# Another machine model for the scheduler that orders a two-block kernel's instructions

## The chip, the cores and the metric

The kernel runs on one core of a Trainium2 chip. The metric is the time of one execution on the device, in microseconds. The three runs shown before the change took 2196.48, 2199.58 and 2181.83 us, with a median of 2196.48.

## The reference

One sequence of 256 tokens with 1024 features goes through two blocks of two layers each. Block 1 puts 16 meta tokens in front (272 in all). Each of its layers computes

```
proj = h @ w_in                       # q k v z b a | sq sk sv | iq ik iw
o_dn = gated_delta_rule(q, k, v, ...) # convolution, chunks, a state passed on
score = sum_h relu(iq_h ik^T) iw_h    # 8 indexer heads
sel   = top_k(causal(score), 64)      # 64 keys for each query
o_sa  = attention of sq over the selected keys, 8 heads
h = layer_norm(a*h + concat(o_dn, o_sa) @ w_out)
h = layer_norm(a*h + moe(h))          # 32 experts, 2 per token
```

Block 2 drops the meta tokens. Each of its layers takes the sum of three gated branches (block-sparse attention with 8 heads, chunked gated linear attention with 4 heads, attention into a memory of 256 tokens), a projection, and an MLP of 4096 with a squared ReLU. All in float32.

## The kernel before

Weights come in from memory as they are used, 414.9 MB for one execution, through the SP queue. Tokens stay on the chip. A product to float32 accuracy is made of three matmuls, L240, L241 and L242: weights and activations are each split into a high and a low part (ScalarE at L232 makes the high part, VectorE at L233 the low one). In block 1 such a product is [128 features x 272 tokens] wide; in block 2 mostly 512.

Block 1, one layer. The projections of q, k, v come first, then the convolution and the delta rule: L932 to L1057 prepare the chunks, with L976 doubling a triangular inverse step by step, and L1067 to L1098 pass the state through them. The indexer's queries and keys are projected and rotated (L496 on TensorE, L499 on VectorE). For two tiles of 128 queries, L522 makes the scores of 8 heads, ScalarE applies the ReLU, and L526 adds them on VectorE. Eight rounds of L531 (the eight largest) and L532 (strike them out) find 64 keys; L533 and L535 turn that into an additive mask, `bias`. The projections of sq, sk and sv, four weights of 256 columns in two pieces each, are written beside the indexer in the program. The sparse heads follow: L627 is the product of queries and keys, L629 adds the mask by a matmul, L630 takes the maximum, L637 and L641 transpose the probabilities, L648 and L650 multiply by the values, and L653 divides by the sums and writes `osa`. In layer 0 the 16 meta tokens have their own heads (L584 to L606). The memory of block 2 is prepared on the side (L1577 on VectorE scales it, L1583 transposes it, L1595 loads its weights).

The expert weights go through three rings of tiles (L1113 loads w1 and w3, eight tiles of 1 MB for a group of four experts; L214 loads w2). The first ring is free during the heads; the second lies where the heads' tiles are, so its loads wait for their end. There are eight groups of four experts a layer: L1186 gathers tokens, L1197 is the first product, L1208 a transpose, L1216 the second product, L1225 scatters.

In block 2, L1783 is a chain of the linear attention: six levels of masks, each of which waits for masked copies on VectorE (L1818) and factors made by ScalarE, VectorE and GpSimd (L1800).

No order of the instructions is written out. The program is a sequence of calls, and the framework's list scheduler puts the instructions of each engine in an order of its own before it places waits between engines. That scheduler picks by a model of the machine. Each engine then executes its list in order, and SP issues the DMAs in its list in order.

Of the kernel before, what the change touches and what calls it, by code (L numbers as in the profile page):

```python
# [15 lines left out]
PSUM = bass.MemoryType.PSUM  # L16
# [4 lines left out]
CAP = 32  # L21
# [19 lines left out]
def _consts():  # L41
    """Tables that depend on the shapes alone: masks, identities, rotary tables of block 1."""
# [64 lines left out]
def build(tc, A, out, dbg=None, stop=None):  # L107
    nc = tc.nc
    es = ExitStack()
    with es:  # L110
# [9 lines left out]
        # the memory's keys and values, and scratch, for the whole run  # L120
        K.pt = es.enter_context(tc.tile_pool(name="mem0", bufs=1, side="right"))
        K.mem = {0: mem_tiles(K, K.pt)}
        for l in range(2):
            with ExitStack() as st:
# [17 lines left out]
                # the expert weights start to come in beside the output projection  # L142
# [5 lines left out]
            with ExitStack() as st:  # L148
                # what dies first lies where the next phase starts
                K.pe = st.enter_context(tc.tile_pool(name="moee%d" % l, bufs=1))  # L150
                K.pf = st.enter_context(tc.tile_pool(name="moef%d" % l, bufs=1))
                K.wc = st.enter_context(tc.tile_pool(name="wringc%d" % l, bufs=RC))
                K.p = st.enter_context(tc.tile_pool(name="moe%d" % l, bufs=1))
                b1_moe(K, l)
# [12 lines left out]
        # block 2: what is needed first lies on the right, where the expert weights were  # L167
# [15 lines left out]
# tiles of the three rings of expert weights; up to which weight of a group the first two serve  # L183
# [20 lines left out]
def wcols(K, w, c0, n=256):  # L204
    """Columns c0.. of a [1024, N] weight as [128, 8, n]."""
# [5 lines left out]
def wrows(K, w, r0, nk=2):  # L211
    """Rows r0.. of a [K, 1024] weight as [128, nk, 1024]."""
# [5 lines left out]
def split(K, x, shape, pool=None):  # L218
    """A float32 weight block of up to 1024 columns as an exact sum of two float32r blocks."""
# [17 lines left out]
def mm3(K, out, a, b, start, stop):  # L237
    """out += a^T b to float32 accuracy; a and b are (high, low) pairs."""
# [6 lines left out]
def put(K, dst, src, sl):  # L245
    """Writes src (PSUM or SBUF) as a high and a low part."""
# [14 lines left out]
def setup(K):  # L261
# [23 lines left out]
    # the convolutions' taps as columns  # L285
# [4 lines left out]
    # a_log, dt_bias on all partitions  # L290
# [14 lines left out]
def feature_columns(K):  # L305
    """The other vectors over features as columns."""
# [9 lines left out]
def to_T(K, src, t):  # L316
    """One token-major tile -> feature-major high and low parts."""
# [10 lines left out]
def row_bank(K, k, tag):  # L328
    """512 features from column k of K.lcol on, along a row that is the same on all partitions."""
# [6 lines left out]
def interleave(gens):  # L336
    """Runs generators in turn, one step of each, until all are done."""
# [9 lines left out]
def yield_from(gen):  # L347
    """Runs a generator to its end and gives what it returns."""
# [7 lines left out]
def b1_attention(K, l, mix, st):  # L356
# [55 lines left out]
    # small columns: db, da, iw  # L412
# [147 lines left out]
    # the memory of block 2 and the first expert weights come in early  # L560
# [13 lines left out]
def b1_sparse_meta(K, sqT, skT, vtok, mix):  # L574
    """The 16 meta tokens, all heads at once."""
# [85 lines left out]
def router_weights(K, l, p):  # L661
    """Router weights with the norm's gain on them, high and low parts; the norm's bias goes with theirs."""
# [19 lines left out]
def b1_project(K, l, mix):  # L682
    """Output projection, residual, layer norm, router logits and choices."""
# [30 lines left out]
    def norm(t, halves):  # L714
        """Residual and norm before gain and bias (left in K.y); feature-major parts of it for the router."""
# [67 lines left out]
def norm_stats(K, y, P, ss, junk, at=0):  # L783
    """Minus the mean and the inverse deviation of y [P, 1024] into ss[:, 2] and ss[:, 5]; ss[:, 0:2] holds the half sums."""
# [16 lines left out]
class Route:  # L801
    """Grouped top-2 routing, one token tile after the other: the expert slots of the tokens and their gates."""
# [26 lines left out]
    def choose(self, t):  # L829
        """The two experts of each token."""  # L830
# [18 lines left out]
    def rank(self, t):  # L849
        """The token's rank among those of the expert."""  # L850
# [9 lines left out]
    def gates(self, t):  # L860
        """Half of the gates of a token tile."""
# [16 lines left out]
class Delta:  # L878
    """Gated delta rule on one token tile: two chunks of 64, or the 16 meta tokens."""
# [12 lines left out]
    def pre(self):  # L892
# [42 lines left out]
        # normalised keys and queries, feature-major  # L935
# [33 lines left out]
        # T = (1 + L)^-1 by block doubling; U its transpose  # L969
# [37 lines left out]
        # token-major keys and values  # L1007
# [101 lines left out]
def moe_load(K, l, g, n):  # L1109
    """Weight n of a group of four experts: w1 of each, then w3 of each."""  # L1110
# [11 lines left out]
def b1_moe(K, l):  # L1122
    """Tokens are gathered into CAP slots per expert; tokens past the slots of an expert take a dense path in a loop
    that only runs when an expert has any."""
# [12 lines left out]
    # the first group's loads began beside the projection  # L1137
# [9 lines left out]
    def onehot(g):  # L1147
        """Token -> slot of a group's experts."""
# [5 lines left out]
    def gates(g, oh):  # L1154
        """The gates there."""
# [4 lines left out]
    def gated(og_):  # L1160
        """Gated slot -> token."""
# [9 lines left out]
    def gain(dst, src, k):  # L1171
        """The first norm's gain and bias of feature block k."""
# [65 lines left out]
    # the meta tokens' sums lie beside them  # L1238
# [3 lines left out]
    def init():  # L1242
        """The residual, of the normed tokens."""
# [30 lines left out]
    # tokens without a slot  # L1274
# [21 lines left out]
def moe_overflow(K, l, ovf, acc, rows, tiles, gain):  # L1296
    """Adds the contribution of the tokens that found no slot, whatever their number."""
# [3 lines left out]
    with tc.If(n > 0):  # L1301
        # tokens feature-major, and the gates of those past the slots
# [45 lines left out]
def setup2(K):  # L1348
    """Per-feature vectors of block 2."""
# [30 lines left out]
def setup2_rest(K):  # L1380
    """Masks, gains on token-major heads, and rotary tables."""
# [872 lines left out]
```

## Time and profile before

| | us |
|---|---|
| runs: median, lowest, highest | 2196.48, 2181.83, 2199.58 |
| the profiled execution: span from first to last instruction | 2178.1 |
| block 1, layer 0: attention; experts | 0 to 316; 325 to 587 |
| block 1, layer 1: attention; experts | 600 to 886; 887 to 1141 |
| block 2, layer 0 | 1148 to 1664 |
| block 2, layer 1 | 1664 to 2178 |

The profile is of one execution. Its own time is not among the three runs; its span lies 3.7 us below the lowest of them and 18.4 below the median. In rows of the trace a busy TensorE is a modelled one: matmuls are pipelined, so what counts is when the next one starts. PEclk is the granted TensorE clock, 1.00 for 2.4 GHz and 0.50 for 1.2.

### The profile page before, as it was taken

To read this page: it belongs to the slowest core of one execution; us is meant where nothing else is said; L and a number is where in the kernel's file an instruction comes from. 1 tells how busy PE (TensorE), PEld (TensorE's weight loads), DVE (VectorE), ACT (ScalarE), POOL (GpSimd) and SP (SyncE) were. 2 spreads that over 40 slices of the span, in tenths; PEclk is the share of its full clock that TensorE was granted. 3 is DMA by queue.
4 is the path that set the end of the run, shared out by engine and by line. 5 is a ranking of instruction groups with operands and counts; after the bars stand their busy time and mean duration, and the time that the engine had idled before them with its cause. 6 is when DMAs were issued, how large, how long until landed. Compare 5 with 4: busy or idle time off the path is not lost. (4 is left out here: it accounts for less than half of the span.)

```text
span 2178.1 us, 34809 instructions
## 1 busy us (share of the span) xinstructions
PE 2037.9 (94%) x14216; PEld 1588.2 (73%) x14216; DVE 1091.5 (50%) x2179; ACT 762.0 (35%) x1478; POOL 358.9 (16%) x342
## 2 busy tenths in 40 slices
PE   8999999999699999988768999999999999999999
PEld 7888665544299887543326779889878869898987
DVE  6658444221376583521116674555545575555554
ACT  5214322111242243211015434455534524445543
POOL 1325000000022430000001130123400031122410
PEclk9999799999899997999889899999999989999999
DMA  7304288999942154999995243254555434244553
GB/s 220 97 20 136 78 290 297 340 356 371 301 132 74 44 187 141 344 368 366 365 335 170 83 166 120 88 184 155 173 194 163 133 116 146 88 153 145 168 193 116
DMA packets 321670, 414.90 MB, mean 190 GB/s; under 512 B 25480, under 2 KB 277970, under 8 KB 321506
## 3 DMA queue, kind: packets, MB, share of 16 engines
q1 hardware_dynamic: 315110, 410.85, 56.4%
q8 instruction: 114, 1.87, 0.4%
q10 hardware_dynamic: 6396, 1.77, 0.3%
q14 instruction: 50, 0.41, 0.1%
HBM read 411.54 MB, written 1.05 MB: 189 GB/s over the span
## 5 line engine op out<-in xcount | busy, mean ns | idle before, releaser
L233 DVE TENSOR_TENSOR wl<-w,wh 128x1024 fp32r<-128x1024 f32 x329 | 411.5, 1253 | 270.8 <-ACT wh L232 263.5
L232 ACT CAST wh<-w 128x1024 fp32r<-128x1024 f32 x350 | 365.7, 1047 | 429.8 <-PE ps_d L241 251.3
L240 PE MATMUL ps_d<-hh,wh 128*128 128x256 f32 (+1 forms) x1632 | 481.7, 296 | 5.5 <-ACT tg L2161 1.9
L242 PE MATMUL ps_d<-hh,wl 128*128 128x256 f32 (+1 forms) x1632 | 475.1, 291 | 0.3
L241 PE MATMUL ps_d<-hl,wh 128*128 128x256 f32 (+1 forms) x1632 | 475.0, 291 | 0.0
L240 PEld LDWEIGHTS ps_d<-hh,wh 128*128 128x128 f32 x1632 | 310.1, 190 | 17.4 <-issue 6.4
L242 PEld LDWEIGHTS ps_d<-hh,wl 128*128 128x128 f32 x1632 | 310.6, 190 | 9.1 <-DVE wl L233 6.9
L241 PEld LDWEIGHTS ps_d<-hl,wh 128*128 128x128 f32 x1632 | 310.1, 190 | 4.7 <-issue 0.8
L1197 PE MATMUL ps_d<-wb,hg 128*32 128x256 f32 x2048 | 156.0, 408 | 33.1 <-DMA wb<-in_w 33.0
L1197 PEld LDWEIGHTS ps_d<-wb,hg 128*32 128x32 f32 x2048 | 73.4, 117 | 106.5 <-DMA wb<-in_w 43.4
L2221 POOL TENSOR_TENSOR relu<-relu 128x256 f32<-128x256 f32 x64 | 86.6, 1354 | 129.6 <-ACT relu L2220 129.6
L1186 PE MATMUL ps_c<-oh,y 128*128 128x128 f32 (+1 forms) x640 | 101.9, 297 | 0.0
L1201 DVE SCALAR_TENSOR_TENSOR mth<-mth,ps_d 128x256 f32<-128x256 f32 x16 | 6.7, 421 | 183.5 <-ACT mth L1200 183.4
L1186 PEld LDWEIGHTS ps_c<-oh,y 128*128 128x128 f32 (+1 forms) x640 | 82.7, 189 | 21.1 <-issue 5.7
L1216 PE MATMUL ps_d<-w,hid 128*32 128x512 f32 x512 | 80.9, 637 | 12.1 <-ACT hid L1210 7.9
L795 POOL TENSOR_TENSOR lnst<-lnst,nhalf 128x1 f32<-128x1 f32 (+1 forms) x5 | 4.9, 980 | 479.7 <-DVE lnst L794 477.8
L1228 DVE TENSOR_TENSOR yacc<-yacc,ps_c 128x512 f32<-128x512 f32 x56 | 38.5, 687 | 83.6 <-PE ps_c L1225 83.6
L1200 ACT ACTIVATE mth<-ps_d 128x256 f32<-128x256 f32 x16 | 6.1, 383 | 211.5 <-PE ps_d L1197 211.5
L233 POOL TENSOR_TENSOR wl<-w,wh 128x1024 fp32r<-128x1024 f32 x21 | 50.0, 2383 | 129.2 <-ACT wh L232 119.8
L2175 POOL TENSOR_TENSOR mergedT<-mergedT,tg 128x256 f32<-128x256 f32 x32 | 32.6, 1041 | 234.0 <-DVE tg L2173 234.0
L1216 PEld LDWEIGHTS ps_d<-w,hid 128*32 128x32 f32 x512 | 21.7, 115 | 60.3 <-issue 36.8
L1225 PE MATMUL ps_c<-ysl,ohT 128*128 128x512 f32 (+1 forms) x140 | 64.5, 603 | 0.0
(679 smaller groups left out, 3686.1 us busy)
## 6 DMA issues: line engine op xcount, KB each, us to landing
wb<-in_w SPq DMA_DIRECT2D x128, 1024.0 KB, 12.0
w<-in_w_in SPq DMA_DIRECT2D x82, 1024.0 KB, 5.3
w<-in_w SPq DMA_DIRECT2D x64, 1024.0 KB, 11.4
w<-in_w_up SPq DMA_DIRECT2D x32, 1024.0 KB, 5.3
w<-in_w_down SPq DMA_DIRECT2D x32, 1024.0 KB, 4.9
w<-in_w_out SPq DMA_DIRECT2D x16, 1024.0 KB, 4.8
w<-in_w_branch SPq DMA_DIRECT2D x24, 512.0 KB, 4.2
w<-in_mem_w_kv SPq DMA_DIRECT2D x8, 1024.0 KB, 5.7
```

Source lines behind the costliest of these rows:

```text
L232: K.nc.scalar.copy(h, x)
L233: eng.tensor_tensor(lo, x, h.bitcast(F32), op=OP.subtract)
L240: PE.matmul(out, a[0], b[0], start=start, stop=False, skip_group_check=True)
L241: PE.matmul(out, a[0], b[1], start=False, stop=False, skip_group_check=True)
L242: return PE.matmul(out, a[1], b[0], start=False, stop=stop, skip_group_check=True)
L1186: PE.matmul(ps[:, (k % 4) * 128:(k % 4) * 128 + 128], y[t][:P, k * 128:(k + 1) * 128], oh[:P, t, :], start=(i == 0), stop=(i == nt - 1))
L1197: PE.matmul(pu[j * 32:j * 32 + 32, i * 256:i * 256 + 256], hg[:, k, j * 32:j * 32 + 32], wts[i][j][:, k, :], start=(k == 0 and i == 0), st ...
L1216: PE.matmul(ps[q * 32:q * 32 + 32, :], hid[:, j, q * 32:q * 32 + 32], w2t[q][:, j, hf * 512:(hf + 1) * 512], start=(j == 0), stop=(j == 1) ...
L1225: PE.matmul(ps[rows[t]], ohT[:, off:off + P], ysl[:, hf * 512:(hf + 1) * 512], start=True, stop=True)
L1228: V.tensor_tensor(sl, sl, ps[rows[t]], op=OP.add)
L2175: G.tensor_tensor(m, m, tg, op=OP.add)
L2221: G.tensor_tensor(r, r, r, op=OP.mult)
```

## The change

The list scheduler takes its times from the framework's detailed simulation of the machine, in place of a simple one. The rest of the diff takes out comments and docstrings; the lines keep their numbers, and no instruction is added or removed on purpose.

```diff
-    with tile.TileContext(nc) as tc:
+    with tile.TileContext(nc, schedule_with_timeline_sim=True) as tc:
         build(tc, A, out)
```

What moves is seen in the order of each engine's list, in nearly all of it. Three places follow, in which x2 means two in a row and "..." rows left out.

**TensorE, layer 0, from the indexer's first scores (L522) to the heads (L627).** Before, the scores stand in eight pairs, each followed by some eight products (L240 to L242) and a rotation (L496), here the first pair and the head of the second:

```order
L522 MATMUL ps_c<-ikT,iqT 128x144 x2
L240 MATMUL ps_d<-hh,wh 128x272
L241 MATMUL ps_d<-hl,wh 128x272
L242 MATMUL ps_d<-hh,wl 128x272
...
L496 MATMUL ps_o<-rraw,cst_750 128x272
...
L522 MATMUL ps_c<-ikT,iqT 128x144 x2
```

Now:

```order
L242 MATMUL ps_d<-hh,wl 128x272
...
L1067 MATMUL ps_c<-state,uw_1285 128x128 x4
L1071 MATMUL ps_p<-state,qd_874 64x128 x4
L1086 MATMUL ps_p<-uw_1285,AT_921 128x128 x4
L1098 MATMUL ps_c<-cst_91,don 128x128 x4
L522 MATMUL ps_c<-ikT,iqT 128x144 x8
L522 MATMUL ps_c<-ikT,iqT 128x272 x8
L1583 MATMUL ps_o<-cst_91,memx 128x128
L1583 MATMUL ps_p<-cst_91,memx 128x128
L553 MATMUL ps_c<-cst_91,rraw 128x128 x2
L553 MATMUL ps_c<-cst_91,rraw 16x128
```

All products that stood between and behind the pairs are now ahead of the first L522, between steps of the delta rule; the last steps of the state (L1067 to L1098) and the sixteen scores stand in one piece. After row L627 come more of the memory's transposes, nine matmuls of the output projection, and then L629 of the first head, in which the mask is added. Layer 1 has the same order, with seven and one of the larger scores.

**VectorE, layer 0, the eight rounds over the larger tile.** Before:

```order
L532 MATCH_REPLACE iacc<-m_2230,iacc 128x272
L531 MAX m_2230<-iacc 128x8
L233 TENSOR_TENSOR wl<-w,wh 128x1024
L532 MATCH_REPLACE iacc<-m_2230,iacc 128x272
...
L233 TENSOR_TENSOR wl<-w,wh 128x1024
...
L533 TENSOR_SCALAR iacc<-iacc 128x272
L535 TENSOR_TENSOR bias_2248<-iacc,cst_750 128x272
L1585 TENSOR_TENSOR memT<-ps_o,lcol 128x512
...
L233 TENSOR_TENSOR wl<-w,wh 128x1024
```

Now:

```order
L531 MAX m_2230<-iacc 128x8
L532 MATCH_REPLACE iacc<-m_2230,iacc 128x272
L533 TENSOR_SCALAR iacc<-iacc 128x272
L535 TENSOR_TENSOR bias_2248<-iacc,cst_750 128x272
L630 TENSOR_REDUCE sst<-ps_d 128x1 x3
L631 TENSOR_SCALAR sst<-sst 128x1 x3
```

Before, weight splitting (L233) stands between the rounds; now nothing of the projections is left there, and L535 is followed directly by the heads' L630 and L631.

**TensorE, block 2, layer 0, inside the chain L1783.** Before:

```order
L1783 MATMUL ps_c<-gX 128x128 x2
L241 MATMUL ps_d<-wl,hh 128x512
L1783 MATMUL ps_c<-gX 128x128 x6
L242 MATMUL ps_d<-wh,hl 128x512
L240 MATMUL ps_d<-wh,hh 128x512
L241 MATMUL ps_d<-wl,hh 128x512
L1783 MATMUL ps_c<-gX 128x128 x2
L242 MATMUL ps_d<-wh,hl 128x512
L1783 MATMUL ps_c<-gX 128x128 x6
```

Now:

```order
L1783 MATMUL ps_c<-gX 128x128 x2
L242 MATMUL ps_d<-hh,wl 24x256
L240 MATMUL ps_d<-hh,wh 24x256
L241 MATMUL ps_d<-hl,wh 24x256
...
L1783 MATMUL ps_c<-gX 128x128 x2
L242 MATMUL ps_d<-hh,wl 24x256
L240 MATMUL ps_d<-hh,wh 24x256
L241 MATMUL ps_d<-hl,wh 24x256
L1783 MATMUL ps_c<-gX 128x128 x2
...
L240 MATMUL ps_d<-wh,hh 128x512 x2
```

Before, up to six matmuls of the chain stand in a row with one to eight of a weight product between; now they stand in twos and fours with three to eleven matmuls of other products between, and the chain begins later in the list.

On the SP queue the expert weights keep their pattern (eight tiles at L1113, then four at L214), with up to two tiles more of L1113 ahead of an L214. The pools and rings are the same.

## Rows read from the trace of the kernel before

**Rows 1.** The page: span, and TensorE's busy us, share, instructions.
```profile
span 2178.1 us, 34809 instructions
...
PE 2037.9 (94%) x14216; PEld 1588.2 (73%) x14216; DVE 1091.5 (50%) x2179; ACT 762.0 (35%) x1478; POOL 358.9 (16%) x342
```

**Rows 2.** Table by stage: stretch, length, busy us per engine (count), granted clock, DMA.
```profile
12.00:172.00 160.00, 152.76 (x1255) 142.08 (x1255) 102.77 (x228) 51.29 (x93) 47.23 (x33) 0.99 0.35 103
172.00:221.00 49.00, 46.78 (x331) 41.13 (x330) 43.26 (x90) 23.30 (x52) 24.52 (x23) 1.00 0.45 153
222.00:243.00 21.00, 21.00 (x124) 14.89 (x123) 10.11 (x35) 9.12 (x33) 0.00 (x0) 0.99 0.41 130
243.00:275.00 32.00, 32.00 (x122) 20.02 (x122) 8.94 (x32) 5.44 (x21) 0.00 (x0) 0.53 0.00 0
325.00:587.00 262.00, 240.50 (x1823) 120.06 (x1822) 71.79 (x164) 35.99 (x86) 2.03 (x2) 0.97 0.98 337
604.00:760.00 156.00, 150.00 (x1226) 140.18 (x1225) 100.59 (x217) 48.28 (x89) 44.10 (x31) 0.98 0.25 77
806.00:826.00 20.00, 20.00 (x118) 14.03 (x116) 9.47 (x34) 8.61 (x32) 0.00 (x0) 1.00 0.78 257
826.00:850.00 24.00, 24.00 (x84) 17.34 (x83) 6.22 (x22) 4.97 (x21) 0.00 (x0) 0.50 0.00 1
886.00:1141.00 255.00, 210.60 (x1704) 103.42 (x1704) 56.47 (x137) 35.67 (x85) 2.03 (x2) 0.93 1.04 358
```

**Rows 3.** Waits of SP's DMA queue, 760 to 870: total us, times, longest.
```profile
SPq L1113 <- DVE osa L653: 36.7, 1, 36.7
```

**Rows 4.** Groups of PE instructions: 172 to 222 us, then 759.6 to 803.
```profile
L240 PE MATMUL ps_d<-hh,wh 128*128 128x272 f32 x88 | 27.0, 307 | 0.0
...
L496 PE MATMUL ps_o<-rraw,cst 128*128 128x272 f32 x16 | 5.7, 435 | 2.2 <-DVE rt L499 1.3 <-ACT rraw L494 0.7
...
L240 PE MATMUL ps_d<-hh,wh 128*128 128x272 f32 x84 | 25.7, 306 | 0.0
```

**Rows 5.** Timelines of PE and DVE, pieces: start us, length us, engine, line.
```profile
170.83 0.29 PE L240 MATMUL ps_d<-hh,wh 128*128 128x272 f32 x1
...
171.83 0.28 PE L242 MATMUL ps_d<-hh,wl 128*128 128x272 f32 x1
172.04 0.52 PE L522 MATMUL ps_c<-ikT,iqT 64*128 64x144 f32 x4
...
174.60 0.53 DVE L526 SCALAR_TENSOR_TENSOR iacc<-irel,wis,cst 128x144 f32<-128x144 f32 x1
...
220.33 0.44 DVE L535 TENSOR_TENSOR bias<-iacc,cst 128x272 bf16<-128x272 f32 x1
...
759.64 0.52 PE L522 MATMUL ps_c<-ikT,iqT 64*128 64x144 f32 x4
...
802.36 0.44 DVE L535 TENSOR_TENSOR bias<-iacc,cst 128x272 bf16<-128x272 f32 x1
```

**Rows 6.** Groups of DVE instructions, 172 to 222 us.
```profile
L233 DVE TENSOR_TENSOR wl<-w,wh 128x1024 fp32r<-128x1024 f32 x9 | 12.1, 1341 | 1.8 <-ACT wh L232 1.8
...
L499 DVE TENSOR_TENSOR rt<-ps_o,cst 128x272 f32<-128x272 f32 x8 | 3.4, 428 | 0.0
```

**Rows 7.** Table by stage: the end of expert layer 0.
```profile
587.00:591.00 4.00, 0.95 (x6) 0.77 (x7) 3.26 (x7) 3.08 (x6) 1.31 (x2) 0.96 1.10 349
591.00:604.00 13.00, 8.92 (x51) 7.37 (x50) 11.36 (x17) 5.51 (x9) 4.15 (x5) 0.50 0.72 181
```

**Rows 8.** Waits of PE, whole span: total us, times, longest.
```profile
PE ps_d L1197 <- DMA wb<-in_w: 33.0, 17, 2.5
...
PE ps_c L1783 <- DVE gAT L1818: 6.1, 6, 1.8
```

**Rows 9.** Table by stage: around the chain L1783 in block 2.
```profile
1239.00:1253.00 14.00, 14.00 (x55) 9.91 (x52) 8.48 (x19) 2.24 (x4) 2.40 (x3) 0.51 0.12 39
1751.00:1762.00 11.00, 11.00 (x39) 7.52 (x37) 7.32 (x16) 2.13 (x4) 2.40 (x3) 0.53 0.01 3
```

## The prediction

> **What bounds the kernel now.** I read the page first: TensorE (PE) is busy 94% of the 2178.1 us span [rows 1], so a new order can do two things only: open or close gaps on PE, and change the clock at which PE runs. That average hides three kinds of stage, so next came the table by stage. The projections, the delta rule and block 2 are limited by PE itself: 152.76 busy of 160 in attention before the indexer, 46.78 of 49 while it runs, 150.00 of 156 in layer 1 [rows 2]. The expert stages are limited by transfers (337 and 358 GB/s at a DMA share of 0.98 and 1.04). Between them stand the sparse heads, a chain of small steps through PE, VectorE (DVE) and ScalarE (ACT), where PE looks fully busy but the granted clock is 0.99 in the first 21 us and 0.53 in the next 32; in layer 1 it is 1.00, then 0.50 [rows 2]. 1.00 is 2.4 GHz and 0.50 is 1.2. DMA is still there (0 and 1 GB/s): the next expert weights go into memory that the heads' tiles hold, and in layer 1 the SP queue waits 36.7 us for the heads' last result [rows 3]. So the end of the heads is on the path: whatever delays it delays the expert loads as well, and those set the length of the next stage.
>
> **Top-k loses its cover.** In the old order the products that score keys (L522) stand in eight pairs between the remaining projections. While DVE takes the 64 best keys, PE works those off. In the new order all of these projections stand before the first L522, between steps of the delta rule. After L522 PE has left only transposes of the memory (L1583, L553), one product per head as far as three banks go, and nine products of the output projection, before L629 needs the mask.
>
> Layer 0, step by step. What moves ahead of L522: three lines of x88, x88 and x89 (one is shown), 265 products, and 16 rope products [rows 4]. Eight products in sequence take from 170.83 to 171.83, that is 0.125 us each [rows 5]: 33.1 us. The ropes are of the same width and overlap their neighbours (5.7 us busy); I count 0.2 each, 3.2. That is 36.3 in all. They are put where PE now has 160 - 152.76 = 7.2 us of idle time [rows 2]; I let them fill all of it. The first L522 comes at 172.04 now [rows 5], hence at 172.0 + 36.3 - 7.2 = 201.1. DVE begins 174.60 - 172.04 = 2.6 us later [rows 5]. DVE is busy 43.26 us from there to the mask [rows 2]; weight splitting (L233, 12.1) and the rotations (L499, 3.4) lie in it now and are gone from it in the new order [rows 6]: 27.8 stay, the rounds L531 and L532 and the memory's L1577 among them, one after another. The mask is ready at 201.1 + 2.6 + 27.8 = 231.5. It is ready now at 220.33 + 0.44 = 220.8 [rows 5]: **+11 us**. Lower end +7, if the memory's part falls into other gaps; upper end +16, if the delta rule's waits stay and the ropes cost all of their 5.7.
>
> Layer 1 has three lines of x84, x84 and x83 between its first L522 at 759.64 and its mask at 802.36 + 0.44 [rows 4, 5]: 251 products, 31.4, and 3.0 for ropes, less 6.0 idle us [rows 2], start L522 at 788.0. With 2.6 + 27.8 the mask comes at 818.4, +16. DVE's chain is some us shorter there (its splitting and the rest fit into 43 us beside it), so I take **+13**; ends 7 and 19.
>
> **The clock of the heads.** Rows show heads starting at 1.00 right after dense products, then falling to 0.50 some 20 us in, and staying there [rows 2]. Elsewhere a stretch with little on PE goes the same way: in the second layernorm 0.95 us busy of 4 is followed by 13 us at 0.50 [rows 7]. In the new order some 20 us with nearly empty PE come just before the heads, so I expect them to begin at 0.50. Price from the rate of instructions: layer 0 has 124 in 21 us at full clock and 122 in 32 at half [rows 2], so 124 at the half-clock rate take 32.5 us, +11.5; layer 1, 118 in 20 and 84 in 24, gives +13.7. The two parts do not hold the same mix, so I take **+10 per layer**. Ends: 0, if the clock stays up, and +20, if the first part doubles.
>
> The Trainium skill, TensorE: Matmul & The Clock Gate, section on HAM oscillation, says that waits which leave the engine idle let its clock fall, so that the next burst starts cold. That speaks against this change. By it the heads begin cold in both layers, and the sum below would be +48, with the upper ends of 20 in place of 10. The trace agrees in the layernorm, where the clock falls to 0.50; no row of it shows heads that begin so.
>
> **Delta rule.** It gets the projections as filler. That gain is already used: the 7.2 and 6.0 idle us above. Its PE work is unchanged.
>
> **Expert stages.** The new order puts the next group's first product (L1197) between the scatter products (L1225), and the SP queue brings w2 as before behind each eight tiles of w1 and w3. The transfers bound the stage, and none is added. I cost it at **0**. Below: layer 0 at layer 1's 358 GB/s would take 262 x 337 / 358 = 246.6, -15 us. Above: PE now executes in order behind a tile that may be late; one wait of about 1 us for each of 16 groups gives +16, which is half as long as the present waits for these tiles, 33.0 us in 17 times [rows 8].
>
> **Block 2.** The chain L1783 waits for DVE (6.1 us for two layers) [rows 8], and its clock drops: 14 us at 0.51 and 11 us at 0.53 [rows 9]. At full clock these would take about 7 and 6, so at most -7 - 3 and -5 - 3 with the waits, **-18** for both. The new order starts it later and puts three to eleven products between every two or four of its own, where six stood in a row. I take -8 each, **-16**; the other end is 0. The rest of block 2 is saturated in both orders.
>
> **Sum.** 11 + 13 for the mask, 2 x 10 for the clock, 0 for the experts, -16 for block 2: +28 on the profiled execution, 2178.1 to 2206. That execution is 18.4 below the median of the three runs, 2196.48, and 3.7 below the lowest, 2181.83. On the median the forecast is 2224.5, **2225 us**.
>
> **Rivals.**
> - *The clock holds.* The nine products and L1583 keep PE awake, or the heads run as now. Then 24 - 16 = +8: 2204, within 1%. For it: the heads of today stay at 1.00 for 20 us with small work. Against: during top-k almost nothing is left for PE. Chance 0.31, which takes in that the new order changes nothing that matters (2196), and a forecast that comes out a little smaller.
> - *Faster: expert loads start inside the heads.* The DMA is idle there for 32 and 24 us [rows 2]. If the new order frees the tiles that those loads wait for before the heads end, the transfer-bound stages that follow shorten by up to 56. With 24 + 20 - 16 that gives -28: 2168. It decides from 50 of those 56 us on (28 + 22), or from 30 on if the clock holds too (8 + 22). Against it: the pools are as before, and the wait is for the heads' own last result [rows 3]. Chance 0.15, and 0.07 for a sum of smaller gains (layer 0's expert stage -15, the clock held, the mask only +7).
> - *The forecast*, slower: 0.47.
>
> About 1% (22 us) is what a measurement tells from no change. Faster by over 1%: 0.22; within: 0.31; slower: 0.47. The range: the ends of all terms together are 14 + 0 - 15 - 18 = -19 and 35 + 40 + 16 + 0 = +91. With the second rival the lower end is -28, 2168. The upper is cut at +70, 2267, since the high ends do not all come together. The forecast's own range is 2205 to 2267.
>
> **What would show it.** Right: in the new trace the larger tile's L535 ends near 231 and 816, PE is nearly empty for 15 to 25 us before, the heads begin at 0.50, the expert loads begin some 20 us later in each layer, and L1783 loses its half-clock stretch. Wrong: a granted clock of 1.00 at the start of the heads; a mask no later than now; expert loads that start before the heads are done; an expert stage longer or shorter by over 15 us.

## The result and the profile after

The changed kernel took 2256.85 us (median of four runs, 2255.80 to 2261.32), the kernel before 2191.97 beside it (2181.83 to 2199.58). The ratio is 1.031, with an interval from 1.027 to 1.035: slower by 65 us, where I had forecast slower by 28. The side was right, the size was not.

The page of the changed kernel: span, TensorE, and the granted clock in 40 slices.

```profile
span 2254.0 us, 34907 instructions
...
PE 2068.6 (92%) x14216; PEld 1612.1 (72%) x14216; DVE 1094.9 (49%) x2179; ACT 763.7 (34%) x1478; POOL 364.6 (16%) x342
...
PEclk9998588998989996799889899999999999999999
```

The number of PE instructions is that of before [rows 1], and PE is busy 31 us longer in a span that is 76 us longer. The 31 are a balance: by the tables further down, block 2 is busy 21 us less, so block 1 is busy 52 us longer, and PE also idles some 46 us longer there. Both count: longer busy time (the 5 and the 6 in the line PEclk lie at the heads of the two layers) and waiting.

The table by stage of the kernel after, with the columns of [rows 2]: layer 0 up to the scores, the top-k, the heads in two parts, the expert groups; then layer 1 up to the heads' second part.

```profile
12.00:214.00 202.00, 191.54 (x1539) 179.79 (x1539) 121.11 (x244) 66.26 (x117) 65.88 (x52) 0.99 0.35 108
214.00:241.00 27.00, 18.66 (x77) 13.45 (x76) 24.38 (x78) 10.41 (x35) 2.38 (x3) 0.69 0.59 195
241.00:262.00 21.00, 19.42 (x62) 11.74 (x61) 6.10 (x25) 6.53 (x23) 0.00 (x0) 0.50 0.00 0
262.00:291.00 29.00, 28.20 (x115) 21.29 (x115) 8.21 (x32) 6.06 (x24) 0.00 (x0) 0.50 0.00 1
...
375.00:631.00 256.00, 233.88 (x1791) 116.15 (x1784) 64.39 (x140) 32.57 (x80) 0.00 (x0) 0.96 0.97 333
```

```profile
656.00:851.00 195.00, 186.44 (x1502) 176.27 (x1503) 115.83 (x233) 62.62 (x110) 64.14 (x49) 0.98 0.30 94
851.00:879.00 28.00, 19.74 (x77) 13.47 (x77) 24.59 (x77) 10.41 (x35) 2.57 (x3) 0.69 0.58 188
879.00:903.00 24.00, 22.48 (x72) 13.74 (x71) 6.76 (x26) 6.90 (x24) 0.00 (x0) 0.50 0.00 1
903.00:923.00 20.00, 19.20 (x70) 14.82 (x70) 5.84 (x22) 5.11 (x21) 0.00 (x0) 0.50 0.00 0
```

Against [rows 2]: while VectorE picks the keys, PE has 77 instructions in 27 us, where it had 331 in 49. The heads begin at a granted clock of 0.50, where they began at 0.99 and 1.00. In layer 0 the clock is 0.50 from 240.5 to 291.7, 51.2 us; before, from 242.6 to 273.3, 30.7 us. In layer 1 it is 44.4 us, and was 23.9.

Milestones in the timelines of after (start us, length us, engine, line): the first scores, the mask and the last head of layer 0, the last expert product of layer 0, and the same of layer 1.

```profile
214.64 3.29 PE L522 MATMUL ps_c<-ikT,iqT 64*128 64x144 f32 x14
240.57 0.44 DVE L535 TENSOR_TENSOR bias<-iacc,cst 128x272 bf16<-128x272 f32 x1
300.64 0.69 DVE L653 TENSOR_TENSOR osa<-ps_o,sst 128x512 f32<-128x512 f32 x1 [4.88 <-PE ps_o L650]
630.26 1.06 PE L1216 MATMUL ps_d<-w,hid 128*32 128x512 f32 x8
851.41 0.85 PE L522 MATMUL ps_c<-ikT,iqT 64*128 64x144 f32 x4
878.52 0.44 DVE L535 TENSOR_TENSOR bias<-iacc,cst 128x272 bf16<-128x272 f32 x1
931.44 0.69 DVE L653 TENSOR_TENSOR osa<-ps_o,sst 128x512 f32<-128x512 f32 x1 [1.17 <-PE ps_o L650]
1233.18 1.02 PE L1216 MATMUL ps_d<-w,hid 128*32 128x512 f32 x2
```

The same of before, where [rows 5] does not have them:

```profile
264.70 0.69 DVE L653 TENSOR_TENSOR osa<-ps_o,sst 128x512 f32<-128x512 f32 x1 [1.81 <-PE ps_o L650]
578.39 1.02 PE L1216 MATMUL ps_d<-w,hid 128*32 128x512 f32 x2
847.93 0.69 DVE L653 TENSOR_TENSOR osa<-ps_o,sst 128x512 f32<-128x512 f32 x1 [2.66 <-PE ps_o L650]
1134.71 1.02 PE L1216 MATMUL ps_d<-w,hid 128*32 128x512 f32 x2
```

The ends of these pieces, after less before, give the terms of the prediction as they came out. In layer 0 the mask is 20.2 later (241.0 against 220.8), the last head 35.9, the last expert product 51.9. In layer 1 the mask is 76.2 later, which is 24.3 more than the 51.9 that it inherits; the last head 83.5, the last expert product 98.5. The span ends 76.0 later.

| term | forecast | in the trace |
|---|---|---|
| mask later | 11 + 13 | 20.2 + 24.3 |
| mask to last head (clock) | 10 + 10 | 15.7 + 7.3 |
| last head to last expert product | 0 + 0 | 16.0 + 15.0 |
| block 2 | -16 | -22.5 |
| sum | +28 | +76.0 |

Waits of SP's queue (layer 1) and of PE (whole span) in after:

```profile
SPq L1113 <- DVE osa L653: 60.3, 1, 60.3
```

```profile
PE ps_d L1216 <- DMA w<-in_w: 48.2, 14, 11.5
PE ps_d L629 <- DVE bias L535: 7.9, 2, 4.0
...
PE ps_d L1197 <- DMA wb<-in_w: 2.8, 2, 1.7
```

The wait for w1 and w3 was 33.0 us in 17 pieces [rows 8] and is nearly gone (2.8); a wait for w2 (the tile `w`) stands in its place, 48.2 us in 14 pieces, which was 4.2 in 6 in the kernel before.

### The profile page after: what moved, and what is told of

Read it like the earlier page. It is cut to its first block, busy times and chain, and to the rows that moved or that the text cites. A ratio compares the mean times of both kernels' runs of the same rounds, so it can differ in the third digit from the quotient of the medians.

```text
span 2254.0 us, 34907 instructions
## 1 busy us (share of the span) xinstructions
PE 2068.6 (92%) x14216; PEld 1612.1 (72%) x14216; DVE 1094.9 (49%) x2179; ACT 763.7 (34%) x1478; POOL 364.6 (16%) x342
## 5 line engine op out<-in xcount | busy, mean ns | idle before, releaser
L233 DVE TENSOR_TENSOR wl<-w,wh 128x1024 fp32r<-128x1024 f32 x329 | 413.4, 1259 | 277.4 <-ACT wh L232 269.6
L240 PE MATMUL ps_d<-hh,wh 128*128 128x256 f32 (+1 forms) x1632 | 471.0, 291 | 8.1 <-ACT G L1733 2.0
L242 PE MATMUL ps_d<-hh,wl 128*128 128x256 f32 (+1 forms) x1632 | 473.7, 291 | 1.1 <-DVE wl L233 0.9
L240 PEld LDWEIGHTS ps_d<-hh,wh 128*128 128x128 f32 x1632 | 304.6, 188 | 15.5 <-issue 3.3
L242 PEld LDWEIGHTS ps_d<-hh,wl 128*128 128x128 f32 x1632 | 306.6, 188 | 10.7 <-DVE wl L233 6.4
L1216 PE MATMUL ps_d<-w,hid 128*32 128x512 f32 x512 | 118.6, 648 | 53.8 <-DMA w<-in_w 48.2
L1197 PE MATMUL ps_d<-wb,hg 128*32 128x256 f32 x2048 | 150.8, 388 | 2.8 <-DMA wb<-in_w 2.8
L1197 PEld LDWEIGHTS ps_d<-wb,hg 128*32 128x32 f32 x2048 | 72.0, 111 | 81.6 <-issue 38.0
L1216 PEld LDWEIGHTS ps_d<-w,hid 128*32 128x32 f32 x512 | 28.0, 115 | 119.3 <-issue 73.3
L1186 PE MATMUL ps_c<-oh,y 128*128 128x128 f32 (+1 forms) x640 | 109.3, 313 | 1.8 <-DVE oh L1150 1.8
L1186 PEld LDWEIGHTS ps_c<-oh,y 128*128 128x128 f32 (+1 forms) x640 | 88.9, 202 | 21.8 <-issue 6.1
L233 POOL TENSOR_TENSOR wl<-w,wh 128x1024 fp32r<-128x1024 f32 x21 | 50.7, 2414 | 144.1 <-ACT wh L232 144.0
L1218 ACT COPY ysl<-ps_d 128x512 f32<-128x512 f32 x32 | 18.7, 585 | 156.1 <-PE ps_d L1216 156.1
L1225 PE MATMUL ps_c<-ysl,ohT 128*128 128x512 f32 (+1 forms) x140 | 70.1, 616 | 0.0
L2175 POOL TENSOR_TENSOR mergedT<-mergedT,tg 128x256 f32<-128x256 f32 x32 | 38.6, 1228 | 182.5 <-DVE tg L2173 182.5
## 6 DMA issues: line engine op xcount, KB each, us to landing
w<-in_w SPq DMA_DIRECT2D x64, 1024.0 KB, 13.7
```

Of the source, the lines that this page charges most:

```text
L233: eng.tensor_tensor(lo, x, h.bitcast(F32), op=OP.subtract)
L240: PE.matmul(out, a[0], b[0], start=start, stop=False, skip_group_check=True)
L242: return PE.matmul(out, a[1], b[0], start=False, stop=stop, skip_group_check=True)
L1186: PE.matmul(ps[:, (k % 4) * 128:(k % 4) * 128 + 128], y[t][:P, k * 128:(k + 1) * 128], oh[:P, t, :], start=(i == 0), stop=(i == nt - 1))
L1197: PE.matmul(pu[j * 32:j * 32 + 32, i * 256:i * 256 + 256], hg[:, k, j * 32:j * 32 + 32], wts[i][j][:, k, :], start=(k == 0 and i == 0), st ...
L1216: PE.matmul(ps[q * 32:q * 32 + 32, :], hid[:, j, q * 32:q * 32 + 32], w2t[q][:, j, hf * 512:(hf + 1) * 512], start=(j == 0), stop=(j == 1) ...
```

## The experiments

My theory after the result: the loss has two sources, in the attention and in the expert stages, and block 2 gains on its own. Within the attention: the projections that went ahead no longer cover VectorE's top-k, and the clock falls. Rivals: the new order of the delta rule costs the time; the parts are not separable; in the experts, either the memory's instructions or the order of the loads.

The hybrids build the program once under each model. Between two marks in the program, each engine then gets the other model's order; everything else is left to the base model. What is left to it need not stay as it was: the list scheduler may place it otherwise, and below it sometimes did.

**One stage at a time.**

```diff
+    pos = order_of(make, True)        # every engine's order under the detailed model
     with tile.TileContext(nc, schedule_with_timeline_sim=False) as tc:
         build_(tc)
+        in_order(tc, pos, at[a], at["end " + b])
+        # new_attention: attn0, attn1   new_experts: moe0, moe1   new_block2: mix20 to mlp21
+        # old_attention: base True, pos of the simple model, attn0, attn1
```

> The old order everywhere, the new order in the attention of block 1 alone (both layers, all engines). Theory A (the loss lies in the attention: the mask comes 20 us later and the heads run at half clock from their start, as the two traces show): each layer's last osa +35, so the kernel is 70 us slower than before, and a little more if the experts' loads are pushed too. Theory B (the loss comes about equally from the expert stages and the output projection, the attention's delay being absorbed behind loads that are not on the path): +30 or less. Theory C (my sum of before): +44.

> The new order everywhere, but the old order in the attention of block 1 (both layers). Theory A: what is left of the change is block 2's gain of 22 us and some loss in the expert stages (9 and 8 us in the traces, if those do not come from the attention): -5 to -22 against before. Theory B: still some 30 to 40 us slower than before.

> The old order everywhere, the new order in the two expert stages alone. My sum of before: 0, since transfers bound the stage. By the traces of the two kernels, if the stages' +9 and +8 us belong to their own order (the wait for w2 at the second product grew from 4.2 to 48.2 us): +17. If they come from the late start after the attention: 0.

> The old order in block 1, the new order in block 2 alone (both layers). By the traces block 2 went from 1027 to 1005 us: -22. My sum of before: -16. If block 2's gain depends on how block 1 leaves the queues: less than -10. If -22 holds, this kernel beats both, by 1%.

Measured beside 2182.25 us of the kernel before: new_attention 2233.92, ratio 1.0235 (1.0167 to 1.0303); old_attention 2203.62, 1.0101 (1.0028 to 1.0174); new_experts 2214.17, 1.0160 (1.0085 to 1.0235); new_block2 2161.42, 0.9897 (0.9831 to 0.9964). The three parts alone are +52, +32 and -21, together +63. The whole change is +65 beside its own runs of the kernel before, and +75 beside these; with intervals of some 15 us to either side of each part, they add up. The attention is the largest part, and the experts, which I had put at 0, are the second. new_attention came out between my sum's +44 and the +70 of theory A; its mask of layer 0 is 20.4 us later, as in the full change. old_attention, +21 us (+6 to +38 by its ratio), lies between its two theories: the experts' loss outweighs the gain of block 2, which theory A had not, but by less than theory B had. new_block2 is 1% faster than the kernel before, with an interval that leaves out 1.

**The lost cover alone.** The simple model's order, but the sixteen scores of a layer are held behind the last product of the projections of sq, sk and sv. The delta rule keeps its old order.

```diff
-                PE.matmul(ps[:, :nk], iqT[...], ikT[...], start=True, stop=True)
+                K.sc.append(PE.matmul(ps[:, :nk], iqT[...], ikT[...], start=True, stop=True))
+    for i in K.sc:                    # K.last: the last projection product
+        K.tc.add_manual_dep(i.ins, K.last.ins.name, NoSync, reason="late")
```

> The old order and the simple model, with one thing forced: the sixteen products that score keys (L522) stand behind the last product of the projections of sq, sk and sv in both attention layers. Theory A (the attention's loss is the cover that top-k lost, with the clock that falls in the gap; how the delta rule is interleaved does not matter): L522 at about 208 us, the mask near 235 to 241, half clock before and through the heads, and the kernel 40 to 55 us slower than before, as with the whole new order of the attention (+52). Theory B (the delta rule's own new order, with fillers used up early and bare steps at its end, costs the larger part): under +25.

Measured: 2229.31 us against 2184.76, ratio 1.0211 (1.0169 to 1.0253). The table by stage of late_scores, layer 0: projections, top-k, first heads.

```profile
172.00:215.00 43.00, 41.69 (x306) 39.74 (x306) 20.63 (x25) 17.92 (x28) 28.13 (x25) 1.00 0.51 175
215.00:238.00 23.00, 14.04 (x79) 9.16 (x78) 20.99 (x73) 8.65 (x31) 0.83 (x1) 0.88 0.48 150
238.00:260.00 22.00, 20.72 (x69) 13.35 (x68) 5.91 (x23) 5.97 (x20) 0.00 (x0) 0.50 0.00 0
```

PE has 79 instructions while VectorE works, and the heads begin at 0.50. The mask of layer 0 comes 17.3 us later, the last head 25.3; the whole is +45 us, where new_attention has +52. At the last expert product of layer 1, ahead of block 2 and its scatter, the two traces are 48.4 and 53.5 us later than before. Behind the heads PE's list is that of before. So one move, in an order that is otherwise the old one, gives nearly all of the attention's loss. That the delta rule's own order costs the larger part is refuted.

**What the clock costs.** Products that nothing uses are put into new_attention where the projections had been. The first try, 40 of them behind the last transpose of v:

```diff
+    for n in range(40):               # behind the last transpose of v, ahead of the first masked head
+        PE.matmul(pt[:, 384:512], K.c["ident"], K.c["ident"], start=True, stop=True)
```

> The kernel with the new order in the attention alone, with 40 products of 128x128 on constants, whose result nobody reads, put on TensorE in the gap between the last transpose of v and the first masked head, in both layers. Theory A (the clock sets the heads' length): the granted clock is back at 1.00 when the heads begin, the heads take some 8 to 12 us less in each layer, and the kernel is 10 to 25 us faster than the one without fill (2234). Theory B (the heads are a chain of waits between engines; the clock is only a mark of that): no gain, or 1 to 4 us a layer lost by the products themselves.

Measured: 2258.07 us against 2184.76, ratio 1.0337 (1.0297 to 1.0377). The table of attention_filled: the filling, and the stretch behind it.

```profile
233.00:242.00 9.00, 9.00 (x82) 9.00 (x81) 0.39 (x1) 0.00 (x0) 0.00 (x0) 1.00 0.00 0
242.00:248.00 6.00, 3.19 (x17) 2.31 (x16) 5.33 (x15) 0.00 (x0) 0.00 (x0) 1.00 0.57 175
```

PE is full and VectorE stands still: 0.39 busy of 9. The products lay ahead of the memory's transposes (L1583); VectorE's copy of those (L1585) stood in front of the top-k rounds in its list, so the mask came at 250.4 instead of 241.2, and the clock was 0.50 again from 248.4 on. The run says nothing of what the clock costs. The second try puts 36 of them behind the last of these transposes:

```diff
+    add_manual_dep(first dummy product, last L1583 of the memory)
+    add_manual_dep(first masked L629, last dummy product)
```

> As new_attention, with 36 more products of 128x128 that nothing uses (L2253) between the last transpose of the memory part and the first masked head, while VectorE makes the mask: they keep PE at work in the place of the projections that went ahead. Theory (part of the attention's loss is the half clock that follows the uncovered stretch): the heads begin at 1.00 near 242 us and the layer's osa comes 8 to 12 us sooner than in new_attention, 2212 to 2220 us in all. Rival (the loss is the mask's lateness alone, the clock falls anyway): 2230 to 2240 us, as new_attention.

Measured: 2221.93 us against 2182.02, ratio 1.0146 (1.0068 to 1.0224). attention_filled2: the top-k's end with the products, then the heads; behind it the first heads of new_attention.

```profile
225.00:240.00 15.00, 15.00 (x108) 12.98 (x106) 14.59 (x47) 3.52 (x16) 0.29 (x1) 0.87 0.58 185
240.00:252.00 12.00, 12.00 (x67) 7.83 (x66) 5.66 (x23) 5.74 (x20) 0.00 (x0) 1.00 0.01 1
252.00:288.00 36.00, 35.73 (x144) 25.51 (x142) 9.65 (x38) 7.59 (x30) 0.00 (x0) 0.51 0.00 1
```

```profile
241.00:256.00 15.00, 13.23 (x41) 7.66 (x41) 4.47 (x18) 4.26 (x15) 0.00 (x0) 0.50 0.00 0
```

The heads begin at 1.00, with 67 instructions in 12 us against 41 in 15. The half-clock stretch of layer 0 shrinks from 51.2 to 37.5 us, by 13.7; at half the rate that is worth 6.9, an estimate. From the mask to the last head it takes 6.2 us less in layer 0 and 8.1 in layer 1, of the 9.6 and 8.1 that new_attention had lost there; the last head of layer 0 comes 7.4 us sooner, the mask's 1.2 included. That is a little under the 8 to 12 expected. In total the kernel is 12 us faster than new_attention by the medians, and 2 us above the range of the theory; the intervals of the two ratios overlap, so the total alone would not decide, and the rows do. They are of one trace each: in seven traces with the old order in the attention this stretch scatters from -4.4 to +4.8 us against before. attention_filled, whose heads begin at 0.50 as in new_attention, lost 11.7 and 8.0 there. The clock is a real part of the attention's loss, about 6 to 8 us a layer of what these products could restore; the mask's lateness remains.

**The experts: memory instructions or loads.** In the new order of new_experts the 32 memory's products of a layer (L1600) are all used up before the tokens of the first group are gathered (L1186), and w2 is issued late. The end of layer 0's list on SP, wb for L1113 and w for L214 (x8: eight tiles; two loads of the memory's weights are left out):

```
before:  wb x8, w x4, wb x8, w x4, wb x8, w x4
now:     wb x8, w x2, wb x8, w x2, wb x7, w x4, wb x2, w x4, wb x1, gb x2, w x4
```

I had described this list as nearly the old one, with up to two tiles more of L1113 ahead of an L214. Counted in the traces it is not: from the third group on, the old order issues w2 right behind its group's eight tiles (one tile later in one group); the new one issues it six tiles later in layer 0 and five in layer 1, up to fourteen in the fifth and sixth group, seven in the seventh, and on time only in the last.

```diff
         in_order(tc, pos, at["moe0"], at["end moe0"])     # and moe1
+        # experts_memory_apart: leaves out the memory's instructions (L1545 to L1600)
+        # experts_loads_alone:  only the instructions of SP
+        # experts_loads_apart:  all engines but SP
+        # experts_both_apart:   leaves out the memory's instructions and SP
```

> The kernel with the new order in the expert stages alone, but the instructions of block 2's memory (L1545 to L1600), which are woven into these stages, are left to the simple model. Theory A (the +32 come from the memory's products: used up while the router waits for VectorE, and with their norm ahead of the first gather, which then runs late and at half clock): back to before, within +-8 us, and the first L1197 of layer 0 near 325 to 330 us. Theory B (the loss comes from L1197 of the next group standing between the scatter products, or from w2 behind more tiles of w1 and w3): still +25 or more.

> The simple model's order everywhere, but for the issues on SP in the two expert stages, which stand in the detailed model's order: the w2 tiles of a group some six to eight w1 and w3 tiles later. Theory (the order of the loads makes the expert groups longer): the last group's last product comes 12 to 17 us later than before in each layer, 25 to 32 us in all, with 5 us stretches under 100 GB/s near the stage's end and long waits of L1216 for the tile w. Rival (the order of the products on PE does it, the loads only follow): under 8 us in all, L1216 not waiting for w.

> As new_experts (the detailed model's order in the two expert stages alone), but the issues on SP in these stages are left to the simple model. Theory (loads' order): the groups are as long as before or shorter, and only the later beginning of the first group is left, which the transfers partly take back: 0 to 15 us over before, where new_experts had 32. Rival (order on PE): again about 25 to 35 us over before.

> As new_experts, but both the memory instructions of block 2 and the issues on SP are left to the simple model, so that of the detailed model's order in the expert stages only that of the expert products and their vector work is left. Theory (the two costs are the uncovered beginning and the loads' order): -5 to +8 us against before. Rival (something else in the order of the products costs too): +15 us or more, with PE waiting in the groups for VectorE or ScalarE and not for DMA.

Measured: experts_memory_apart 2208.15 us against 2184.76, ratio 1.0123 (1.0061 to 1.0184). Beside 2182.02 us: experts_loads_alone 2217.78, 1.0162 (1.0079 to 1.0246); experts_loads_apart 2229.30, 1.0217 (1.0127 to 1.0306); experts_both_apart 2195.55, 1.0054 (1.0004 to 1.0105). From the traces, against before, in us for layer 0 and layer 1: how much longer it takes from the last head to the first L1197, and from there to the last L1216.

| kernel | to the first expert product | the eight groups |
|---|---|---|
| new_experts | +16.3, +12.4 | +3.5, +5.8 |
| experts_memory_apart | -0.1, +1.1 | +12.5, +17.6 |
| experts_loads_alone | +1.0, +0.3 | +13.1, +15.8 |
| experts_loads_apart | +16.1, +12.4 | +9.9, +7.3 |
| experts_both_apart | +0.1, +1.1 | +8.2, +8.0 |
| the full change | +13.7, +8.9 | +2.3, +6.0 |

In four traces with the old order in these stages and another attention or block 2 (new_attention, new_block2 and the two with filling), the groups take -1.9 to +0.1 us, so the second column stands clear of the scatter.

The first column is settled: it is +9 to +16 where the memory's instructions have the new order and 0 to 1 where they have not. experts_memory_apart has its first product of layer 0 at 325.2, as theory A had it, but in total +23 us, where theory A allowed 8. Rows of new_experts, before the first expert product and behind it, and of experts_memory_apart and the kernel before for the same stretch:

```profile
320.00:325.00 5.00, 1.61 (x8) 1.18 (x8) 2.83 (x7) 0.91 (x2) 1.99 (x2) 0.87 1.02 402
325.00:344.00 19.00, 19.00 (x87) 13.36 (x89) 3.11 (x19) 4.33 (x15) 0.00 (x0) 0.50 0.01 5
```

```profile
325.00:345.00 20.00, 20.00 (x194) 12.81 (x194) 12.27 (x44) 5.21 (x17) 2.03 (x2) 1.00 0.33 109
```

```profile
325.00:344.00 19.00, 19.00 (x188) 11.94 (x188) 14.12 (x45) 4.75 (x16) 0.00 (x0) 1.00 0.74 245
```

In new_experts PE is nearly empty in front of the gather, and the clock is 0.50 for the 19 us that follow: 87 instructions, where there were 188. The DMA stands at 5 GB/s there: SP waits 25.4 us for the first product, which frees tiles of its ring (12.7 before). With the memory's instructions left to the old model this is gone. The gather of layer 0 in the kernel before, then in new_experts with what stands in front of it:

```profile
316.65 8.60 PE L1186 MATMUL ps_c<-oh,y 128*128 128x128 f32 x48
```

```profile
323.61 1.04 PE L1545 MATMUL ps_o<-cst,msq 128*128 128x128 f32 x4 [3.39 <-DVE msq L1559]
325.40 15.19 PE L1186 MATMUL ps_c<-oh,y 128*128 128x128 f32 x48
```

So the delay has two parts. The gather begins 9.7 us later behind the last head, 11.5 in layer 1: ten of the memory's products (twelve in layer 1) and those of its norm (L1545), which stood behind the gather, are now ahead of it, with a wait of 3.4 us for VectorE. And at 0.50 the gather itself takes 15.1 us to the first product in place of 8.5; in layer 1 that is 4.6 in place of 3.7.

The second column has at least two causes. In experts_loads_alone nothing but the order of the issues on SP is forced, and its groups are 13 and 16 us longer, within what that theory expected; in total it is +36, somewhat more than its 25 to 32. PE's list did not stay the same, though: the scheduler moved products with the loads, for one the memory's second 32, which stand in one piece from 480.6 to 494.5 and stood in two from 446.2 to 465.4. So the run does not change the loads alone. What speaks for them is the wait for w2. Waits of PE from 320 to 640 in experts_loads_alone, in experts_loads_apart, and the DMA in the first:

```profile
PE ps_d L1216 <- DMA w<-in_w: 17.0, 6, 9.2
```

```profile
PE ps_d L1197 <- DMA wb<-in_w: 20.8, 8, 5.6
```

```profile
570.00:580.00 10.00, 9.41 (x97) 5.03 (x96) 0.82 (x2) 1.76 (x4) 0.00 (x0) 1.00 0.46 165
590.00:600.00 10.00, 8.76 (x48) 3.20 (x46) 2.21 (x7) 2.31 (x5) 0.00 (x0) 1.00 0.31 100
```

The long wait for w2 comes and goes with SP's order: in layer 0 it is 13 to 17 us in the four kernels with the new list, 0.7 before, and none in the two whose list on SP is left to the scheduler. But experts_loads_apart did not come out as expected (0 to 15): it is +47 by the medians, more than its rival's 25 to 35 too. Its groups wait for w1 and w3 instead, and the late first product is still there. Even with both left out, experts_both_apart keeps 8 us a layer, with PE waiting for w1 and w3 (33.2 us in layer 1's stretch from 870 to 1190, against 25.3 before). Its ratio, +1 to +23 us, lies between what the two theories expected and excludes neither. Nor do these two kernels have the old list on SP: the scheduler issues w2 of the sixth and seventh group three and two tiles later than before. The pieces also don't add: when the first product is late by 16 us anyway, the groups lose 3.5 and not 13 behind it. What I can say: the memory's instructions cost 9 to 16 us a layer ahead of the first product; the new order of the loads, with the shifts on PE that came with it, 13 to 16 where nothing else is late; and with neither forced the new order of the products leaves some 8. How the last 8 arise is not settled, and how much of the 13 to 16 is the loads by themselves is not shown.

## Why the prediction was wrong

**The step that failed.** "... the SP queue brings w2 as before behind each eight tiles of w1 and w3. The transfers bound the stage, and none is added. I cost it at **0**." By the table above, the full change lost 31 us there: 22.6 between the last head and the first expert product, 8.3 in the groups. The larger part lies in the stretch of 60 us in layer 0 and 42 in layer 1 in front of the groups, which I did not cost at all: the memory's products, which had been spread over it and beyond, stand in one piece ahead of the router (330.6 to 346.0 in layer 0). The gather begins 7.0 and 7.2 us later behind the last head, and takes 6.7 and 1.7 us longer. The smaller part is in the step itself. The order on SP was not as before: from the third to the seventh group, w2 stands behind five or more tiles of w1 and w3 of later groups. Where nothing else is late, that and what moved with it is worth 13 to 16 us a layer; in the full change, where the first product is late anyway, little of it is added. A stage that transfers bound is not safe from a new order if the order of the transfers changes too. My upper end for the stages was +16, for both layers together.

**The second step, mis-sized.** "They are put where PE now has 160 - 152.76 = 7.2 us of idle time [rows 2]; I let them fill all of it." They filled none. PE idles 202.00 - 191.54 = 10.5 us ahead of L522 in after, where it had 7.2 [rows 2]; in layer 1 195.00 - 186.44 = 8.6, where it had 6.0. The products were put between steps of the delta rule, but not into its waits. L522 came at 214.6, not 201.1, and the mask at 241.0, not 231.5. VectorE's part was shorter than I had it: 26.4 from L522 to the mask, where I had 2.6 + 27.8. (The 27.8 was itself misread: rows 6 run to 222 and hold a ninth weight splitting that lies behind the mask, so 29.0 stay by these rows.) The prediction named the opposite case ("if the delta rule's waits stay") as an end of +16; with busy time 2.5 us above my 36.3 it was 20.2. In layer 1 L522 is 39.9 us later beyond what was inherited, where I had 28.4, and the mask 24.3, above my end of 19.

**The clock.** The direction was right: the heads begin at 0.50 in both layers. The price of 10 a layer was 15.7 and 7.3 in the trace, 23 in place of 20. In layer 0 not all of the 15.7 is the clock: new_attention, with the same 51.2 us at 0.50, has 9.6. The full change has more of the output projection between the heads: 32 products for the meta tokens (L711) and 18 of L240 to L242 stand there up to the last head, where new_attention has 5 and 6. That these make the other 6 us is likely, but no run moves them alone. Groups of PE instructions from the mask to the last head, in after (241 to 300.6) and in new_attention (241.2 to 294.7):

```profile
L711 PE MATMUL ps_d<-w,mixm 128*16 128x256 f32 x32 | 3.9, 383 | 0.0
```

```profile
L711 PE MATMUL ps_d<-w,mixm 128*16 128x256 f32 x5 | 1.0, 387 | 0.0
```

The Trainium skill, TensorE: Matmul & The Clock Gate, section on HAM oscillation, says that waits let the clock fall and that the next burst starts cold. The heads of after agree, at 0.50 in both layers. Of the two prices that the prediction set beside each other, 10 and 20 a layer, the traces are nearer to 10: the stretch at 0.50 grew by 20.5 us in each layer of after, and the heads took 9.6 us longer in layer 0 of new_attention and 7.3 in layer 1 of after.

**Block 2.** -16 was forecast and -22.5 came, but the reason was half wrong. I had counted shorter waits in L1783 beside the clock. These waits did go (8.0 us before, 0.6 after), but the chain itself became longer. Tables of before (the chain of layer 0, all of block 2), of after, and of new_experts, which has the old order here:

```profile
1228.00:1265.00 37.00, 32.92 (x192) 23.01 (x194) 28.08 (x66) 9.11 (x17) 14.04 (x16) 0.82 0.20 66
...
1151.00:2178.00 1027.00, 996.69 (x6570) 867.40 (x6568) 575.77 (x944) 472.26 (x845) 197.21 (x202) 0.97 0.44 144
```

```profile
1329.00:1374.00 45.00, 44.58 (x300) 31.72 (x299) 35.91 (x72) 16.46 (x24) 13.93 (x18) 1.00 0.55 176
...
1249.00:2254.00 1005.00, 975.49 (x6570) 857.40 (x6570) 584.35 (x945) 471.53 (x847) 206.13 (x203) 0.99 0.46 147
```

```profile
1266.00:1298.00 32.00, 27.91 (x204) 19.57 (x206) 29.02 (x69) 9.73 (x17) 14.73 (x17) 1.00 0.28 90
```

With 300 instructions in place of 192, the chain takes 45 us, but at a clock of 1.00, and what it took in is missing later. PE idles 30 us in block 2 in both. The old order at full clock needs 32 us for the chain, as in the trace of new_experts. So the gain is for the most part the clock, and how large it is depends on the execution it is measured against. Block 2 took 1007.8 to 1030.3 us in ten profiled executions of the old order (mean 1023.0), and 1004.9, 1005.7 and 1008.2 in three of the new one. In it the clock was 0.50 for 53.6 us on the mean with the old order and for 28.9 with the new one; at half the rate the 24.7 us are worth 12.3, an estimate, of a mean difference of 16.7. What the other 4 us are is open. That 16.7 is so near to the forecast is in part luck, since the profile of before was among the slower ones, and the sum counted waits whose end left PE's idle time as it was.

**The rivals.** "The clock holds" fell: 0.50 in the heads. "Expert loads start inside the heads" fell: the DMA moved 0 to 1 GB/s in them, as in their second part before, and SP's wait for the last head grew from 36.7 [rows 3] to 60.3 us. My sign that would show the prediction wrong, an expert stage longer by over 15 us, came about in layer 0 and was just missed in layer 1, with 16.0 and 15.0 from the last head on.

## What to carry to other kernels

When a scheduler's order changes, read every engine's list for what has been moved ahead of the steps that are limited by another engine: work that is free to move is worth most as cover for those, and using it up early costs twice, in the wait and in the clock behind it. Read the DMA issuer's list to its end as well, above all in a stage that transfers bound. When an experiment forces the order on one engine, compare the lists of the others too: what is left to the scheduler can move along, and then the run shows more than one cause. And take the new order only where it pays: the new order in block 2 alone took 2161.42 us, ratio 0.9897 (0.9831 to 0.9964), against 1.031 for the whole change.

## What the runs showed of the hardware

The same order does not always get the same clock: the chain L1783 of layer 0, with the old order, took 37 us at 0.82 in one execution and 32 at 1.00 in another (rows above), and this may be a large part of the scatter of the kernel before, 2166 to 2201 us over its runs here: block 2 alone, with one order on PE, spread over 22 us in ten traces, and its time at 0.50 from 21.4 us in the shortest to 67.7 in the longest. Half of that difference, an estimate of its price, is 23. The runs of new_block2 spread over 8 us.

VectorE's instructions took different times for the same shape. The group of L526 in before, from 172 to 221, and in after, from 214 to 241:

```profile
L526 DVE SCALAR_TENSOR_TENSOR iacc<-irel,wis,iacc 128x144 f32<-128x144 f32 (+1 forms) x14 | 9.0, 645 | 0.4
```

```profile
L526 DVE SCALAR_TENSOR_TENSOR iacc<-irel,wis,iacc 128x144 f32<-128x144 f32 (+1 forms) x14 | 6.9, 494 | 1.0 <-ACT irel L525 0.3
```

GpSimd was busy 24.52 of 49 us in the first stretch [rows 2] and 2.38 of 27 in the second. In late_scores, where it was busy 0.83 of 23, the same group took 426 ns each. No run here takes GpSimd's work away alone, so that this is the cause is not shown.
